# 512-column products in two feed-forward parts, five table blocks held in the gates' buffer, and new row and request rates in a three-layer transformer kernel

## The chip, the cores and the metric

One core of one Trainium2 chip runs the whole program in one launch. The metric is the device time of that core in microseconds (us); lower is better.

## The reference, cut to what matters

256 tokens of width 1024 pass through three blocks: a convolution and attention mix followed by a layer of 16384 small experts (called peer), then an attention mix with a feed-forward part, then a gating and attention mix with a second feed-forward part. All of it is float32. Of the parts the change touches:

```python
def chunk(args):
    hx, idx, g = args
    a = jax.nn.gelu(jnp.einsum("ced,cd->ce", u_emb[idx], hx), approximate=False)
    return jnp.einsum("ce,ced->cd", g * a, v_emb[idx])
...
h = _rmsnorm(x, norm_ffn[layer])
gu = h @ ffn_w_gu[layer]
x = x + (jax.nn.silu(gu[..., :FFN_HIDDEN]) * gu[..., FFN_HIDDEN:]) @ ffn_w_down[layer]
```

Each token has 128 chosen experts (8 heads, 16 each); u_emb and v_emb have 16384 rows of 1024. FFN_HIDDEN is 2816, which is 22 chunks of 128.

## The kernel before, in words

**Products.** Activations are kept with features on the partitions, a chunk being 128 features by 256 tokens. A weight tile of 128x1024 (512 KB, `raw`) holds eight 128x128 blocks. ScalarE rounds it to `whi` (line 150), VectorE (line 157) or, early in the program, GpSimd (line 155) takes the remainder `wlo`. The activations are split in the same way into a high and a low tile. `mm_t` (lines 176 to 178) makes three products of 256 columns for each block: `whi` with the high activations, `whi` with the low ones, `wlo` with the high ones, all summed in one PSUM tile. The program has four such PSUM tiles (`mm`) and four others (`ax`). `token_major` (lines 242 to 244) is the other way round: 128 tokens are the stationary operand and 512 columns of a weight tile stream past.

**Feed-forward parts** (`ffn`, one per later layer). For each of 22 chunks f the kernel makes two such sums of eight blocks, the gate `pg` and the up part `pu`. Then `act` scales both by the norm `rb` from PSUM (lines 1421 and 1423), applies Silu on ScalarE (1422), multiplies (1424) and splits the result into `ah` and `al` (387, 388). The first part multiplies by the down weights in `residual`, eight sums of 22 blocks each; the second uses `token_major`, in `finish`. Weights come by DMA from SyncE's queue (SP), line 130.

**The peer layer.** The first 160 tokens are computed densely: all 128 blocks of the first table `ut` (line 1054, 16 matmuls a block, `ublock`), gelu into a buffer G, a product of one-hot matrices placed over G by `place` and `put` (lines 1092, 1102), then all 128 blocks of the second table `vv` (line 1162, 16 matmuls a block, `vmm`), the upper 64 first. G is two tiles of 64 x 160 columns. For the last 96 tokens, in two groups (`RowGroup`, 64 and 32 indices wide), GpSimd gathers rows: 96 indirect DMAs of 512 KB from `un` (the first table), each followed by a dot product on VectorE (line 1653), and 96 from `vv`, each followed by a scaled addition (line 1663). Eight row buffers serve them, so a gather waits until the arithmetic on the row eight before it is done. `some_rows(r)` advances the gathers by r per table block: `RU` per block of the first table, `RV` per block of the second.

**Where blocks live.** The first eight `ut` blocks go to the row buffers, asked for by ScalarE before the stage. The others go through a ring of ten 512 KB buffers (`whole`, line 1042), in order of a running number, and SP asks for each as soon as the buffer's earlier block has been multiplied. Of the second table's blocks every fourth by that number is asked for by GpSimd instead, in GpSimd's program order among the gathers; the first of them is the very first block of the second table. The order of this stage on each engine is the order in which the code is written (`in_order`).

Of the kernel before, what the change touches and what calls it, by code (L numbers as in the profile page):

```python
# [9 lines left out]
F32 = mybir.dt.float32  # L10
F32R = mybir.dt.float32r
# [3 lines left out]
AF = mybir.ActivationFunctionType  # L15
# [7 lines left out]
T = 256  # L23
D = 1024
C = D // 128
# [57 lines left out]
QP = 2.8  # L83
UP = (1.5, 1.3)

RU = 0.85
RV = 0.78

AL = 1
GL = (4, 6, 8)  # L90
# [3 lines left out]
N = ROWS[-1][0]  # L94

RB = 8


class Kernel:
# [80 lines left out]
    def wblocks(self):  # L180
        while True:
            for hi, lo in self.blocks(1):
                for b in range(8):
                    yield hi, lo, b

    def mm_tile(self):
        return self.pp.tile([128, T], F32, name="mm", bufs=4)

    def chunk(self, xs, kc=8, order=None):
        pt = self.mm_tile()  # L190
        self.mm_t(self.wb, xs, order or range(kc), pt, (True, True))
        self.tick()
        return pt
# [35 lines left out]
    def token_major(self, xs, kc, n, last=1, first=None, each=None):  # L229


        nc = self.nc
        xh, xl = xs
        pts = [self.pp.tile([128, n], F32, name="mm", bufs=4) for _ in range(2)]
        per = 1024 // n

        def part(tt, t0, hi, lo):
            for j in range(per):
                k = t0 * per + j
                s = slice(j * n, (j + 1) * n)  # L240
                ts = slice(tt * 128, (tt + 1) * 128)
                nc.tensor.matmul(pts[tt], xh[:, k, ts], hi[:, s], start=(k == 0), stop=False)  # L242
                nc.tensor.matmul(pts[tt], xl[:, k, ts], hi[:, s], start=False, stop=False)  # L243
                nc.tensor.matmul(pts[tt], xh[:, k, ts], lo[:, s], start=False, stop=(k == kc - 1))  # L244

        nt = kc // per
        for t0 in range(nt - last):
            (hi, lo), = self.blocks(1)
            for tt in range(2):
                part(tt, t0, hi, lo)  # L250
            self.tick()
            if each:
                each()
        ends = list(self.blocks(last))
        for tt in range(2):
            for t0, (hi, lo) in enumerate(ends):
                part(tt, nt - last + t0, hi, lo)
            if tt == 0 and first:
                first(pts[0])
        for _ in ends:  # L260
            self.tick()
        return pts
# [138 lines left out]
        self.later(1, scale)  # L401
        self.later(2, rows)

    def residual(self, pool, chunk, old, g):

        nc = self.nc
        x = pool.tile([128, C, T], F32, name="x")
        xh = pool.tile([128, C, T], F32R, name="xgh")
        xl = pool.tile([128, C, T], F32R, name="xgl")
        rb = pool.tile([128, T], F32, name="rb")  # L410
        r = self.token_scale()
        step, sums = self.squares(pool, "sq")
        for c in range(C):
            pt = chunk(c)
            nc.vector.tensor_add(x[:, c], pt, old[:, c])
            nc.scalar.activation(xh[:, c], x[:, c], AF.Copy, scale=self.p(g, c))
            nc.vector.scalar_tensor_tensor(xl[:, c], x[:, c], self.p(g, c), xh[:, c], op0=ALU.mult, op1=ALU.subtract)
            step(c, x[:, c])
        self.norm_later(r, rb, sums, D)
        return x, (xh, xl), r, rb  # L420


    def attention(self, pairs):
# [418 lines left out]
    def peer(self):  # L842
        nc, a = self.nc, self.a
        p2h, p2t, p2q = self.p2h, self.p2t, self.p2q
        x, xs, r, rb = self.x, self.xs, self.r, self.rb
# [18 lines left out]
        pr = self.open("rows", side="right")  # L864
        first = [pr.tile([128, D], F32, name="row", bufs=RB) for _ in range(RB)]
        for i, raw in enumerate(first):
# [101 lines left out]
        for h in range(8):  # L968
            for c in range(2):
                pt = self.chunk(xs)  # L970
# [52 lines left out]
        pg = self.open("pg", side="right")  # L1023
        Gs = [pg.tile([128, 64, N], F32, name="G0")]
# [4 lines left out]
        def some_rows(n):  # L1029
            nonlocal owed  # L1030
            owed += n
            while owed >= 1.0:
                owed -= 1.0
                next(fetch, None)

        ring = ["raw", "whi", "wlo", "raw", "whi", "wlo", "raw", "whi", "wlo", "raw"]

        def whole(src, n, eng=nc.sync):

            name = ring[n % len(ring)]  # L1040
            raw = self.sp.tile([128, 1024], F32, name=name, bufs=ring.count(name))
            eng.dma_start(raw, src)
            return raw
# [4 lines left out]
        muls = []  # L1048

        def ublock(i, n_t):  # L1050
            raw = first[i] if i < RB else whole(a["ut"][i], i - RB)
            pt = self.pp.tile([128, N], F32, name="mm", bufs=4)
            for k in range(C):
                nc.tensor.matmul(pt, raw[:, k * 128:(k + 1) * 128], hn[:, k, :N], start=(k == 0), stop=(k == C - 1))  # L1054
            self.tick()
            if n_t == 0:
                nc.scalar.activation(G(i), pt, AF.Gelu)
            else:
                ac = pg.tile([128, N], F32, name="ac", bufs=3)
                nc.scalar.activation(ac[:, :n_t], pt[:, :n_t], AF.Gelu)  # L1060
                if n_t < N:
                    nc.scalar.activation(G(i, slice(n_t, N)), pt[:, n_t:], AF.Gelu)
                muls.append((G(i, slice(0, n_t)), ac[:, :n_t]))
# [45 lines left out]
        k = next((k for k, u in enumerate(self.bg) if k and u not in firsts), len(self.bg))  # L1109
# [4 lines left out]
        i = 0  # L1114
        while self.bg or self.lag:
            ublock(i, 0)
            self.pump(UP[len(asked)])
            if asked:
                some_rows(RU)
            i += 1  # L1120
# [9 lines left out]
        for g in range(n_g):  # L1130
            if g + 2 < n_g:
                ohs.append(onehots(4 * (g + 2), poh, io))
            while i < i0 + 1 + (g + 1) * (126 - i0) // n_g:
                ublock(i, 4 * done)
                some_rows(RU)
                products(1)
# [5 lines left out]
        while i < 128:  # L1142
            ublock(i, 4 * done)
            if pts:
                put(4 * done, i + 1, pts.pop(0))
                done += 1
            some_rows(RU)
            products(1)
# [15 lines left out]
        for q in range(4):  # L1164
            for k in range(4):
                nc.tensor.matmul(acc[q].rearrange("p a b -> p (a b)")[:, k * 128:(k + 1) * 128], zero, zero, start=True, stop=False, skip_group_check=True)
        nv = 128 - RB
        for i in range(64, 128):

            blk = (i, whole(a["vv"][i], nv, nc.gpsimd if nv % 4 == 0 else nc.sync))  # L1170
            nv += 1
            for d in range(8):
                vmm(blk, d)
            some_rows(RV)
        self.close("pgb")
# [3 lines left out]
        xh = p3h.tile([128, C, T], F32R, name="xgh")  # L1179
        xl = p3h.tile([128, C, T], F32R, name="xgl")  # L1180
        rb = p3h.tile([128, T], F32, name="rb")
        for i in range(64 - LAST):

            blk = (i, whole(a["vv"][i], nv, nc.gpsimd if nv % 4 == 0 else nc.sync))
            nv += 1
            for d in range(8):
                vmm(blk, d)
            some_rows(RV)
        for _ in fetch:
# [40 lines left out]
        r1, r2, r = self.token_scale(), self.token_scale(), self.token_scale()  # L1230
# [177 lines left out]
    def ffn(self, name):  # L1408
        nc = self.nc
        x, xs, rb = self.x, self.xs, self.rb  # L1410
        pf = self.open(name, side=self.side)
        if name == "ffn0f":
            self.odd_rows(pf)
        F = 22
        ah = pf.tile([128, F, T], F32R, name="ah")
        al = pf.tile([128, F, T], F32R, name="al")

        def act(f, pg, pu):
            g = pf.tile([128, T], F32, name="g", bufs=3)
            u = pf.tile([128, T], F32, name="u", bufs=3)  # L1420
            nc.vector.tensor_mul(g, pg, rb)
            nc.scalar.activation(g, g, AF.Silu)
            nc.vector.tensor_mul(u, pu, rb)
            nc.vector.tensor_mul(u, u, g)
            self.split(u, ah[:, f], al[:, f])

        last = name == "ffn1f"
        xt = pf.tile([128, 2, D], F32, name="xt") if last else None

        def turn(tt, half):  # L1430

            pt = self.pp.tile([128, 4, 128], F32, name="ax", bufs=4)
            for k in range(4):
                nc.tensor.transpose(pt[:, k], x[:, 4 * half + k, tt * 128:(tt + 1) * 128], self.ident)
            nc.scalar.activation(xt[:, tt, half * 512:(half + 1) * 512], pt.rearrange("p a b -> p (a b)"), AF.Copy)

        for f in range(F):
            pg = self.chunk(xs)
            pu = self.chunk(xs)
            self.after_norm(lambda f=f, pg=pg, pu=pu: act(f, pg, pu))  # L1440
            if last and f in (8, 10, 12, 14):
                turn(f % 4 // 2, (f - 8) // 4)
        self.flush()
        if last:
            self.finish(pf, (ah, al), F, xt)
            return
        nh = self.next_head(name + "h")
        self.x, self.xs, self.r, self.rb = self.residual(nh, lambda c: self.chunk((ah, al), F), x, "mix1")
        self.dump("x5", self.x)
        self.close(name)  # L1450
        self.close(self.head)
        self.head = name + "h"
# [217 lines left out]
def fetched(groups):  # L1670
# [4 lines left out]
    begun = []  # L1675
    for g, f, s in todo + [(None, 0, 0)] * (RB - 1):
        if g is not None:
# [193 lines left out]
```

## Time and profile before

| what | value |
|---|---|
| median of three runs | 1575.03 us (1572.44 to 1576.2) |
| the profiled execution, its time | 1572.59 us |
| its span | 1570.7 us |
| TensorE busy, share of the span | 1520.5 us, 97% |
| VectorE busy | 1111.3 us, 71% |
| ScalarE busy | 647.5 us, 41% |
| GpSimd busy | 546.5 us, 35% |
| HBM read | 395.04 MB |

PE stands for TensorE's matmuls, DVE for VectorE, ACT for ScalarE, POOL for GpSimd, SP for SyncE, which only asks for transfers. Matmuls overlap in the pipeline, so a busy share of PE near 100% says that it was never empty, and its pace is read from the starts of matmuls that follow each other. In this execution the peer tables are worked on from about 318 to 931 us, the first feed-forward part's gates lie around 1150 us, and the second part's around 1450 us.

### The profile page before, as it was taken

The page shows a single profiled execution, that of the slowest core. Times are in us where ns is not written, and L with a number is a line of the kernel's source. Part 1 is how long each engine was busy: PE and PEld are TensorE (multiplying, and loading weights), DVE is VectorE, ACT ScalarE, POOL GpSimd, SP SyncE. Part 2 cuts the span into 40 slices and gives each one's busy share as a digit, 9 for nine tenths or more (in the row PEclk, how much of TensorE's full clock was granted, in tenths as well). Part 3 has the DMA queues.
Part 4 walks back from the last instruction along what each step waited for, and adds up shares of the span by engine and source line. Part 5 has one row for each costly group of instructions (what it writes and reads, how often), then busy time and mean ns, then how long its engine had stood idle before and what let it go on. Part 6 is the DMA issues. An engine that isn't in the chain of part 4 may idle for free.

```text
span 1570.7 us, 30113 instructions
## 1 busy us (share of the span) xinstructions
PE 1520.5 (97%) x11514; PEld 1462.8 (93%) x11514; DVE 1111.3 (71%) x2510; ACT 647.5 (41%) x1398; POOL 546.5 (35%) x593
## 2 busy tenths in 40 slices
PE   9999988999999998999899999999999999999997
PEld 8988987999999998999899999889999997899986
DVE  6989876979998998544344449777776558776655
ACT  4588454422355542000000034565544446655543
POOL 4957804704587776655455301000000030000000
PEclk9999999999999999999999999999999999999999
DMA  6534547449999999999999955626656586365563
GB/s 201 172 116 128 169 144 277 149 160 366 409 408 408 408 408 405 396 409 409 410 409 408 408 181 184 215 94 197 193 183 187 180 204 190 124 196 177 177 191 115
DMA packets 109680, 399.18 MB, mean 254 GB/s; under 512 B 12516, under 2 KB 12931, under 8 KB 109024
## 3 DMA queue, kind: packets, MB, share of 16 engines
q1 hardware_dynamic: 72720, 262.18, 48.2%
q0 software_dynamic: 35232, 130.64, 21.8%
q10 hardware_dynamic: 1584, 4.45, 0.8%
q8 instruction: 90, 1.47, 0.4%
q14 instruction: 54, 0.44, 0.1%
HBM read 395.04 MB, written 6.11 MB: 255 GB/s over the span
## 4 chain that ended last, share of the span: by engine, by line
PE 81%; DMA 10%; DVE 4%; issue 2%; POOL 1%; ACT 1%; ACTq 0%; POOLq 0%; DVEq 0%
PE mm L1054 17%; PE mm L176 14%; PE mm L178 13%; PE mm L177 13%; PE ax L1162 12%; DMA row<-vv,idx 3%; DMA whi<-vv 2%; DMA raw<-wst 2%; PE mm L244 2%; PE mm L243 2%; PE mm L242 2%; POOL wlo L155 1%; PE ax L1092 1%; DMA wlo<-vv 1%; DVE wlo L157 1%
## 5 line engine op out<-in xcount | busy, mean ns | idle before, releaser
L150 ACT ACTIVATE whi<-raw 128x1024 fp32r<-128x1024 f32 x275 | 290.5, 1059 | 604.4 <-PE ax L1162 281.9
L157 DVE TENSOR_TENSOR wlo<-raw,whi 128x1024 fp32r<-128x1024 f32 x213 | 262.5, 1235 | 115.0 <-ACT whi L150 110.9
L178 PE MATMUL mm<-xgh,wlo 128*128 128x256 f32 x1064 | 302.5, 284 | 3.7 <-DVE wlo L157 3.7
L176 PE MATMUL mm<-xgh,whi 128*128 128x256 f32 x1064 | 305.6, 287 | 0.0
L177 PE MATMUL mm<-xgl,whi 128*128 128x256 f32 x1064 | 302.1, 284 | 0.0
L1663 DVE SCALAR_TENSOR_TENSOR acc<-row,w,acc 128x1024 f32<-128x1024 f32 x94 | 120.8, 1285 | 153.1 <-DMA row<-vv,idx 152.8
L178 PEld LDWEIGHTS mm<-xgh,wlo 128*128 128x128 f32 x1064 | 204.9, 193 | 4.3 <-DVE wlo L157 3.9
L155 POOL TENSOR_TENSOR wlo<-raw,whi 128x256 fp32r<-128x256 f32 x248 | 180.4, 762 | 80.7 <-ACT whi L150 80.4
L176 PEld LDWEIGHTS mm<-xgh,whi 128*128 128x128 f32 x1064 | 204.8, 193 | 2.2 <-issue 1.5
L177 PEld LDWEIGHTS mm<-xgl,whi 128*128 128x128 f32 x1064 | 204.9, 193 | 0.2
L1648 POOL DMA_INDIRECT row<-vv,idx x96 | 127.0, 1323 | 99.7 <-DMA row<-vv,idx 71.0
L1162 PE MATMUL ax<-G,raw 128*128 128x160 f32 x816 | 122.2, 303 | 7.1 <-DMA raw<-vv 7.1
L1648 POOL DMA_INDIRECT row<-un,idx x96 | 110.6, 1153 | 38.6 <-DVE a L1653 18.3
L1162 PEld LDWEIGHTS ax<-G,raw 128*128 128x128 f32 x816 | 115.4, 193 | 7.4 <-DMA raw<-vv 7.4
L1653 DVE CUSTOM_DVE_ANT_0 junk<-row,h 128x1024 f32<-128x1024 f32 x96 | 120.0, 1250 | 0.4
L1054 PE MATMUL mm<-hn,raw 128*128 128x160 f32 x768 | 112.6, 300 | 0.0
L1054 PEld LDWEIGHTS mm<-hn,raw 128*128 128x128 f32 x768 | 106.3, 190 | 0.0
L177 PE MATMUL mm<-hl,whi 128*128 128x256 f32 x368 | 104.3, 283 | 0.0
L1162 PE MATMUL ax<-G,whi 128*128 128x160 f32 x624 | 95.9, 304 | 6.8 <-DMA whi<-vv 6.7
L630 DVE SCALAR_TENSOR_TENSOR ax<-u,cw,ax 128x256 f32<-128x256 f32 x227 | 99.3, 483 | 1.6 <-ACT ax L628 0.8
L1162 PEld LDWEIGHTS ax<-G,whi 128*128 128x128 f32 x624 | 89.6, 194 | 7.5 <-DMA whi<-vv 7.5
L1162 PE MATMUL ax<-G,wlo 128*128 128x160 f32 x608 | 90.8, 301 | 2.5 <-DMA wlo<-vv 2.5
(437 smaller groups left out, 3302.7 us busy)
## 6 DMA issues: line engine op xcount, KB each, us to landing
raw<-wst SPq DMA_DIRECT2D x278, 512.0 KB, 3.7
raw<-ut SPq DMA_DIRECT2D x48, 512.0 KB, 15.7
raw<-vv SPq DMA_DIRECT2D x38, 512.0 KB, 7.9
whi<-ut SPq DMA_DIRECT2D x36, 512.0 KB, 16.0
wlo<-ut SPq DMA_DIRECT2D x36, 512.0 KB, 15.7
whi<-vv SPq DMA_DIRECT2D x33, 512.0 KB, 7.8
wlo<-vv SPq DMA_DIRECT2D x26, 512.0 KB, 7.9
raw<-vv POOLq DMA_DIRECT2D x13, 512.0 KB, 17.0
```

Of the source, the lines that this page charges most:

```text
L150: nc.scalar.activation(hi, raw, AF.Copy)
L155: nc.gpsimd.tensor_sub(lo[:, p], raw[:, p], hi[:, p])
L157: self.pin = nc.vector.tensor_sub(lo, raw, hi)
L176: nc.tensor.matmul(pt, w[:, s], xs[0][:, k], start=first, stop=False)
L177: nc.tensor.matmul(pt, w[:, s], xs[1][:, k], start=False, stop=False)
L178: nc.tensor.matmul(pt, lo[:, s], xs[0][:, k], start=False, stop=last)
L630: nc.vector.scalar_tensor_tensor(y[:, c] if k == 30 else ps, u[:, c, k:k + T], cw[:, c, k:k + 1], ps, op0=ALU.mult, op1=ALU.add)
L1054: nc.tensor.matmul(pt, raw[:, k * 128:(k + 1) * 128], hn[:, k, :N], start=(k == 0), stop=(k == C - 1))
L1162: nc.tensor.matmul(acc[d // 2][:, d % 2, :N], raw[:, d * 128:(d + 1) * 128], G(i), start=False, stop=False, skip_group_check=True)
L1648: self.k.nc.gpsimd.indirect_dma_start(t, None, table, bass.IndirectOffsetOnAxis(ap=self.idx[:, s:s + 1], axis=0))
L1653: self.k.nc.vector.tensor_tensor_reduce(junk, row, self.h, 1.0, 0.0, ALU.mult, ALU.add, self.a[:, s:s + 1])
L1663: self.k.nc.vector.scalar_tensor_tensor(self.acc, row, w, self.acc, op0=ALU.mult, op1=ALU.add)
```

## The change

Four edits. In the feed-forward parts the high and low activations lie side by side (`both`), and `chunk_wide` makes, for each weight block, one product of 512 columns (`whi` with both halves) and one of 256 (`wlo` with the high half). The low half's sum then stands in its own 256 columns of the PSUM tile, and is added behind: by a ScalarE copy and a VectorE addition for `pg` and for `pu`, and by one more VectorE addition for each down chunk of the first part. The second part's `finish` is as before. In the peer layer, blocks 27 to 31 of the first table are asked for by ScalarE at block 2 and lie in the upper half of the first G tile, which is written only from block 32 on; the ring's running number skips them. `RU` goes from 0.85 to 0.90 and `RV` from 0.78 to 0.73. GpSimd asks for no block among the second table's first ten; with the new numbers its first is block 13 of that table.

```diff
-RU = 0.85
-RV = 0.78
+RU = 0.9
+RV = 0.73
 RB = 8
+XB = range(27, 27 + 32 * N // D)
...
+    def chunk_wide(self, xs, kc=8):
+        nc = self.nc
+        pt = self.pp.tile([128, 2, T], F32, name="mm", bufs=4)
+        for k in range(kc):
+            w, lo, b = next(self.wb)
+            s = slice(b * 128, (b + 1) * 128)
+            nc.tensor.matmul(pt.rearrange("p a b -> p (a b)"), w[:, s], xs[2][:, k].rearrange("p a b -> p (a b)"),
+                             start=(k == 0), stop=(k == kc - 1), skip_group_check=True)
+            nc.tensor.matmul(pt[:, 0], lo[:, s], xs[0][:, k], start=False, stop=(k == kc - 1), skip_group_check=True)
+        self.tick()
+        return pt
+    def both(self, pool, n):
+        x = pool.tile([128, n, 2, T], F32R, name="xhl")
+        return x[:, :, 0], x[:, :, 1], x
...
-    def residual(self, pool, chunk, old, g):
+    def residual(self, pool, chunk, old, g, wide=False):
...
+            if wide:
+                nc.vector.tensor_add(old[:, c], pt[:, 1], old[:, c])
+                pt = pt[:, 0]
             nc.vector.tensor_add(x[:, c], pt, old[:, c])
...
+        hold = Gs[0].rearrange("p i t -> p (i t)")[:, 32 * N:]
+        nb = 0
...
-            raw = first[i] if i < RB else whole(a["ut"][i], i - RB)
+            nonlocal nb
+            if i < RB:
+                raw = first[i]
+            elif i in XB:
+                raw = hold[:, (i - XB[0]) * D:(i - XB[0] + 1) * D]
+            else:
+                raw = whole(a["ut"][i], nb)
+                nb += 1
+            if i == 2:
+                for j in XB:
+                    nc.scalar.dma_start(hold[:, (j - XB[0]) * D:(j - XB[0] + 1) * D], a["ut"][j])
...
-        nv = 128 - RB
+        nv = nb
         for i in range(64, 128):
-            blk = (i, whole(a["vv"][i], nv, nc.gpsimd if nv % 4 == 0 else nc.sync))
+            blk = (i, whole(a["vv"][i], nv, nc.gpsimd if nv % 4 == 0 and i >= 64 + len(ring) else nc.sync))
...
-            nc.vector.tensor_mul(g, pg, rb)
+            nc.scalar.activation(g, pg[:, 1], AF.Copy)
+            nc.vector.tensor_add(g, pg[:, 0], g)
+            nc.vector.tensor_mul(g, g, rb)
             nc.scalar.activation(g, g, AF.Silu)
-            nc.vector.tensor_mul(u, pu, rb)
+            nc.scalar.activation(u, pu[:, 1], AF.Copy)
+            nc.vector.tensor_add(u, pu[:, 0], u)
+            nc.vector.tensor_mul(u, u, rb)
             nc.vector.tensor_mul(u, u, g)
...
-            pg = self.chunk(xs)
-            pu = self.chunk(xs)
+            pg = self.chunk_wide(xs)
+            pu = self.chunk_wide(xs)
```

Where the two tables meet, GpSimd's order before is this (`un` and `vv` behind `row` are the tables of the gathers, `R` is a one-hot product, and `raw`, `whi`, `wlo` are ring buffers that take blocks of the second table):

```order
L1082 TENSOR_TENSOR R<-QO,gTl 128x512
L1648 DMA row<-un,idx_4404 128x1024 x6
L1648 DMA row<-vv,idx_4395 128x1024
L1042 DMA raw<-vv 128x1024
L1648 DMA row<-vv,idx_4395 128x1024 x3
L1042 DMA whi<-vv 128x1024
```

and after the change this:

```order
L1688 DMA row<-un,idx_4403 128x1024 x2
L1119 TENSOR_TENSOR R<-QO,gTl 128x512
L1688 DMA row<-vv,idx_4394 128x1024 x16
L1069 DMA wlo<-vv 128x1024
L1688 DMA row<-vv,idx_4394 128x1024 x3
L1069 DMA wlo<-vv 128x1024
```

Before, one gather from the second table stood ahead of GpSimd's first block; now sixteen stand there.

In the first feed-forward part, one chunk f on VectorE read before (`wlo` is a weight remainder, `mm` a PSUM sum, `rb` the norm):

```order
L1421 TENSOR_TENSOR g_12577<-mm_12515,rb_11054 128x256
L157 TENSOR_TENSOR wlo_12620<-raw_12617,whi_12619 128x1024
L1423 TENSOR_TENSOR u_12578<-mm_12546,rb_11054 128x256
L1424 TENSOR_TENSOR u_12578<-u_12578,g_12577 128x256
L157 TENSOR_TENSOR wlo_12659<-raw_12656,whi_12658 128x1024
L388 TENSOR_TENSOR al_11299<-u_12578,ah_11298 128x256
```

and now reads:

```order
L1458 TENSOR_TENSOR g_12233<-mm_12187,g_12233 128x256
L1459 TENSOR_TENSOR g_12233<-g_12233,rb_11047 128x256
L158 TENSOR_TENSOR wlo_12307<-raw_12304,whi_12306 128x1024
L1462 TENSOR_TENSOR u_12234<-mm_12210,u_12234 128x256
L1463 TENSOR_TENSOR u_12234<-u_12234,rb_11047 128x256
L1464 TENSOR_TENSOR u_12234<-u_12234,g_12233 128x256
L158 TENSOR_TENSOR wlo_12330<-raw_12327,whi_12329 128x1024
L408 TENSOR_TENSOR xhl_11291<-u_12234,xhl_11291 128x256
```

Two additions from PSUM have joined the six operations of a chunk, and the order of the others is the same.

On ScalarE the five new requests stand near the start of the first table (`G` is the buffer, line 1094 the gelu of a block):

```order
L1094 ACT_TABLE_LOAD
L1094 ACTIVATE G_4391<-mm 128x160 x2
L1088 DMA G_4391<-ut 128x1024 x5
L1094 ACTIVATE G_4391<-mm 128x160 x14
L1019 ACT_TABLE_LOAD
```

They come behind the gelu of blocks 0 and 1 and ahead of that of block 2.

## Rows read from the trace of the kernel before

**Rows 1.** The page: the span, and the busy time of two engines.
```profile
span 1570.7 us, 30113 instructions
...
PE 1520.5 (97%) x11514; PEld 1462.8 (93%) x11514; DVE 1111.3 (71%) x2510; ACT 647.5 (41%) x1398; POOL 546.5 (35%) x593
```

**Rows 2.** Timeline of PE in the first feed-forward part: start us, length us, what.
```profile
1150.11 0.28 PE L176 MATMUL mm<-xgh,whi 128*128 128x256 f32 x1
...
1150.47 0.28 PE L176 MATMUL mm<-xgh,whi 128*128 128x256 f32 x1
```

**Rows 3.** Timeline of PE in the last product, 512 columns a matmul.
```profile
1528.41 0.39 PE L242 MATMUL mm<-whi,ah 128*128 128x512 f32 x1
...
1529.09 0.39 PE L242 MATMUL mm<-whi,ah 128*128 128x512 f32 x1
```

**Rows 4.** Groups by line on DVE, 1115 to 1195 us: count | busy us, mean ns.
```profile
L157 DVE TENSOR_TENSOR wlo<-raw,whi 128x1024 fp32r<-128x1024 f32 x28 | 34.3, 1225 | 9.3 <-ACT whi L150 8.4
...
L1421 DVE TENSOR_TENSOR g<-mm,rb 128x256 f32<-128x256 f32 x14 | 6.0, 425 | 4.1 <-PE mm L178 4.1
```

**Rows 5.** Timeline of DVE in the same place, with the idle time before each.
```profile
1151.75 0.42 DVE L1421 TENSOR_TENSOR g<-mm,rb 128x256 f32<-128x256 f32 x1 [0.29 <-PE mm L178]
1152.77 1.23 DVE L157 TENSOR_TENSOR wlo<-raw,whi 128x1024 fp32r<-128x1024 f32 x1 [0.60 <-ACT whi L150]
1154.63 0.42 DVE L1423 TENSOR_TENSOR u<-mm,rb 128x256 f32<-128x256 f32 x1 [0.63 <-PE mm L178]
...
1157.51 0.42 DVE L1421 TENSOR_TENSOR g<-mm,rb 128x256 f32<-128x256 f32 x1 [0.29 <-PE mm L178]
```

**Rows 6.** Windows in the peer layer: busy us by engine, PE clock, DMA share, GB/s.
```profile
326.00:341.00 15.00, 15.00 (x114) 15.00 (x114) 13.79 (x58) 4.69 (x11) 0.61 (x2) 1.00 0.01 2
...
371.00:381.00 10.00, 10.00 (x76) 10.00 (x75) 9.24 (x45) 1.44 (x5) 4.06 (x6) 1.00 1.02 408
...
620.00:640.00 20.00, 12.87 (x83) 12.62 (x82) 17.33 (x25) 0.59 (x3) 12.40 (x11) 0.83 0.99 378
890.00:904.00 14.00, 14.00 (x104) 14.00 (x104) 6.42 (x5) 0.00 (x0) 2.02 (x2) 1.00 1.03 408
```

**Rows 7.** Waits of PE from 612 to 932 us: total us, times, longest.
```profile
PE ax L1162 <- DMA raw<-vv: 7.1, 1, 7.1
PE ax L1162 <- DMA whi<-vv: 6.7, 2, 4.1
PE ax L1162 <- DMA wlo<-vv: 2.5, 2, 1.8
```

**Rows 8.** The chain of waits from 560 to 910 us: start us, length us, what.
```profile
603.13 4.40 PE mm L1054 x32
607.53 0.46 PE ax L1092 x8
...
618.55 12.57 DMA raw<-vv
...
872.42 17.35 DMA wlo<-vv
...
889.81 20.28 PE ax L1162 x146
```

**Rows 9.** The page, DMA issues: count, KB each, median us from issue to landing.
```profile
raw<-ut SPq DMA_DIRECT2D x48, 512.0 KB, 15.7
raw<-vv SPq DMA_DIRECT2D x38, 512.0 KB, 7.9
...
raw<-vv POOLq DMA_DIRECT2D x13, 512.0 KB, 17.0
```

**Rows 10.** Timeline of PE in the second table, one block and the next.
```profile
843.10 2.34 PE L1162 MATMUL ax<-G,wlo 128*128 128x160 f32 x16
845.27 1.52 PE L1162 MATMUL ax<-G,raw 128*128 128x160 f32 x10
```

**Rows 11.** Groups by line on DVE, 450 to 610 us: the row dot products.
```profile
L1653 DVE CUSTOM_DVE_ANT_0 junk<-row,h 128x1024 f32<-128x1024 f32 x57 | 69.4, 1217 | 0.0
```

More of the change, by code (lines that the diff above doesn't have):

```diff
@@ L232, in token_major @@
         nc = self.nc
-        xh, xl = xs
+        xh, xl = xs[:2]
         pts = [self.pp.tile([128, n], F32, name="mm", bufs=4) for _ in range(2)]
@@ L402, in norm_later @@
         self.later(2, rows)
-    def residual(self, pool, chunk, old, g):
+    def residual(self, pool, chunk, old, g, wide=False):
         nc = self.nc
         x = pool.tile([128, C, T], F32, name="x")
-        xh = pool.tile([128, C, T], F32R, name="xgh")
-        xl = pool.tile([128, C, T], F32R, name="xgl")
+        xh, xl, xb = self.both(pool, C)
         rb = pool.tile([128, T], F32, name="rb")
@@ L419, in residual @@
         self.norm_later(r, rb, sums, D)
-        return x, (xh, xl), r, rb
+        return x, (xh, xl, xb), r, rb
     def attention(self, pairs):
@@ L1414, in ffn @@
         F = 22
-        ah = pf.tile([128, F, T], F32R, name="ah")
-        al = pf.tile([128, F, T], F32R, name="al")
+        ah, al, ab = self.both(pf, F)
         def act(f, pg, pu):
@@ L1447, in ffn @@
         nh = self.next_head(name + "h")
-        self.x, self.xs, self.r, self.rb = self.residual(nh, lambda c: self.chunk((ah, al), F), x, "mix1")
+        self.x, self.xs, self.r, self.rb = self.residual(nh, lambda c: self.chunk_wide((ah, al, ab), F), x, "mix1", True)
         self.dump("x5", self.x)
```

## The prediction

> **What bounds the kernel now.** I read the page first: PE is busy 97% of the span [rows 1]. So time can be gained where PE's own work shrinks, or where PE waits. Two stretches matter, and a different view answers for each.
>
> In the feed-forward parts the timeline of PE is a comb without gaps. The first of three products of one weight block starts at 1150.11 and the first of the next block at 1150.47 [rows 2], so three products of 256 columns take 0.360 us, 0.120 each. PE is the limit there, and only a smaller bill for PE helps. The last product of the kernel already streams 512 columns: three starts lie between 1528.41 and 1529.09 [rows 3], 0.227 us each. That is less than twice 0.120. Solved for a price per column and one per matmul, the two spacings give 0.417 ns a column and 13.3 ns for each instruction.
>
> In the peer layer the windows show transfers that hardly run from 326 to 341 us (2 GB/s) while PE multiplies blocks it already has, and then 408 GB/s from 371 on [rows 6]. A block or a gathered row is 512 KB, 0.524 MB, so one takes 0.524/408 = 1.285 us of all transfers: I call that a unit. The waits of PE by line are 16.3 us, all on blocks of the second table [rows 7]: 7.1 on its first block and 9.2 later. The chain of waits says which blocks: the first was asked for only at 618.55 and took 12.57 us; the last such wait ends at 889.81, for a block asked for at 872.42 that took 17.35 us [rows 8]. Those are GpSimd's: a block that SP asks for lands in 7.9 us, one that GpSimd asks for in 17.0 [rows 9], with gathers queued ahead of it.
>
> **The change part by part.**
>
> *512-column products.* A weight block costs 0.227 + 0.120 = 0.347 us of PE in place of 0.360. Gates and up parts have 2 x 22 x 2 x 8 = 704 blocks, the first part's down product 8 x 22 = 176, together 880. 880 x 0.0133 = **11.7 us**. Bounds: nothing is gained if a 512-column product costs two of 256 here; the weight block is swapped at every matmul in both combs, so I take the measured 0.227. The Trainium skill ("TensorE: Matmul & The Clock Gate", section "Back-to-back issue gap") gives N/2.4 + 2.5 ns for a warm gap, which would make the saving 2.5 ns a block, 2.2 us in all. It speaks against this change, but it would put 256 columns at 109 ns and 512 at 216, and the rows have 120 and 227, so I go by the rows.
>
> *What this adds on ScalarE and VectorE.* A chunk f lasts 5.76 us now (1151.75 to 1157.51 [rows 5]) and 16 x 0.347 = 5.55 after. VectorE works 2 x 1.225 + 4 x 0.425 = 4.15 us in it [rows 4] and gets two more additions of that size: 5.00 of 5.55. ScalarE has two weight roundings and two small operations, and gets two copies; it stays well under VectorE. So both hide under PE, by 0.55 us on VectorE. If that cover went, every 0.1 us of a longer round would cost 44 x 0.1 = 4.4 us. VectorE now idles 0.29, 0.60 and 0.63 us a round at three points [rows 5], waiting for PE and ScalarE; those waits are slack of an engine that is ahead, and should be filled. The eight extra additions of the down product lie in chunks of 22 x 0.347 = 7.6 us and cost nothing; the one behind the last chunk is covered by seven weight blocks of the next product.
>
> *Five blocks held.* ScalarE asks for them behind the gelu of block 1, at about 322 us (two blocks of 2.2 us after the table begins). Five requests hold ScalarE up for a few us; four PSUM tiles of 2.2 us each cover that. The transfers, 5 x 1.285 = 6.4 us, fall into the idle window up to 341 us. From 371 us on the transfers have 6.4 us less to bring. While blocks 27 to 31 are used no ring buffer comes free, so SP asks for nothing for 11 us; gathers and the 15.7 us that a block of this table is in flight [rows 9] keep the transfers busy, narrowly. **6.4 us** less transfer, which counts only if transfers set the end.
>
> *They do.* With PE alone the second table costs 845.27 - 843.10 = 2.17 us a block [rows 10], 8.7 us for four. Four blocks and 4 x 0.78 rows are 7.12 units, 9.15 us: transfers are slower, and PE's lead is eaten until it waits. After the change four blocks and 4 x 0.73 rows are 6.92 units, 8.89 us, still over 8.7, and still at 408 GB/s at 890 to 904 us [rows 6].
>
> *Row rates.* 0.05 more for some 112 blocks of the first table is six gathers earlier, and six fewer later. In the first table two blocks and the one-hot products behind them take PE 4.40 + 0.46 us [rows 8], 2.43 us a block; 1.90 units are 2.44 us. So the first table now needs all transfers, and the 6.4 us of blocks held pay for the six rows (7.7 us). VectorE does 57 dots of 1.217 us in 160 us there with no wait ahead of them [rows 11]; three to four more are 4 to 5 us, which I take to fit. Cost: nothing, but no gain either except through the next step.
>
> *SP asks for the first ten.* The 7.1 us wait at the seam goes: SP can ask for the first block as soon as a buffer is free, some 20 us before it is needed. The transfers lost 20 x (1 - 378/408) = **1.5 us** there [rows 6]. What is late next is GpSimd's first block, now block 13: sixteen gathers stand ahead of it, of which 13 x 0.73, nine to ten, come after the seam. At 1.285 us each with SP's blocks between them, up to 2.57 us, GpSimd asks some 12 to 25 us after the seam and the block lands 17 us later, 29 to 42; PE wants it after 13 x 2.17 = 28. So the wait moves to block 13, 1 to 14 us.
>
> *What the peer layer gains.* As transfers are busy all the time, such waits do not add up; the end follows from what must be delivered before GpSimd's last late block. That was block 112 with seven gathers behind it (landed 889.81); it becomes block 113, also with seven behind it. One more block to deliver, one block less of PE's work behind it: 2.17 - 1.285 = 0.9 us. Sum 6.4 + 1.5 + 0.9 = **8.8 us**. Bounds: nothing (the new wait starves the transfers as long as the old one did, and the held blocks are lost) and 16.3 (all waits gone).
>
> **Sum.** 11.7 + 8.8 = 20.5 us. The profiled execution took 1572.59 us (span 1570.7), so 1552.1; its time lies 2.4 us under the median of the runs shown, 1575.03, so the median should be **1554.5 us**, 1.3% less.
>
> **The rivals.**
> 1. *GpSimd's block 13 is too late, and it is not made up.* While PE waits, SP's ring is full, only eight gathers are in flight, and each new one needs POOL. If 5 to 6 us of transfer time are lost there, the peer layer gives 3 us: 1560. For it: the sixteen gathers; against: eight gathers are 10 us of queued transfers. 15%.
> 2. *All waits vanish*, because rows and blocks now balance: 16.3 + 11.7, 1547. Against: 8.89 is over 8.7. 7%.
> 3. *The held blocks come when transfers are busy* (ScalarE late), or SP's pause lets the transfers run dry: 6.4 us less gain, 1561. 5%.
> 4. *The wide product costs as much as two*, so that edit does nothing: 0 to 2.2 us instead of 11.7, 1564 to 1566. The two combs speak against it. By the formula of the Trainium skill cited above it would be 1564. 4%.
> 5. *VectorE sets the feed-forward round: slower than before.* If its 1.52 us of waits [rows 5] stay where they are, because each new addition waits for a ScalarE copy that waits for PE, a round is 5.00 + 1.52 = 6.52 us, 0.97 over PE's 5.55, and 44 rounds lose 43 us: 1597. It decides from 5.55 on, and the whole change turns slower from 5.55 + 20.5/44 = 6.02 us a round. Against: those waits are an idle engine's, and a late VectorE meets its inputs ready; the weight remainders are made two tiles ahead. 3% for slower than before, and 7% for a round between 5.55 and 6.02 (1556 to 1574).
>
> **How the numbers follow.** My forecast has 59%: 1551 to 1558 by the spread of the runs shown and the 1.5 and 0.9 us terms. The range 1546 to 1564 takes in rivals 1 to 3 and the upper part of 5, some 85%. A measurement of this kernel can tell about 0.2%, 3 us, from no change. Faster by more than that: the forecast, rivals 1 to 4 and most of the 7%, 0.94. Within: 0.02. Slower: rival 5 and what I don't see, 0.04.
>
> **What would show it.** In the profile after: starts in the gates alternating 0.227 and 0.120, no idle PE there, VectorE near 90% in that stretch; transfers at work between 326 and 341 us; no wait at the seam, a wait before block 13, and the later waits smaller; the second table's end near 922 us instead of 931, and the first part's gates about 5 us shorter. A round of VectorE over 5.55 us with PE waiting, or a second table that ends at 928 or later, would prove the matching term wrong.

## The result, and the profile after

The changed kernel takes 1563.98 us (median of 5 runs, 1562.55 to 1566.71) beside 1576.2 us of the kernel before in the same runs: ratio 0.9934, 95% interval [0.9918, 0.995]. By the ratio that is 10.4 us less (7.9 to 12.9), by the two medians 12.2; the forecast was 20.5. The profiled execution took 1563.79 us, 8.8 under that of before.

The page:
```profile
span 1562.0 us, 28572 instructions
...
PE 1517.8 (97%) x10634; PEld 1414.2 (91%) x10634; DVE 1138.7 (73%) x2606; ACT 665.3 (43%) x1486; POOL 542.8 (35%) x590
```
Matmuls are 880 fewer than in [rows 1], one for each block, but PE's busy time fell by only 2.7 us; two steps of the sum have to be looked at apart.

**The gates.** Windows of the kernel after in the first part's gates (busy us of PE, PEld, DVE, ACT, POOL, then clock, DMA share, GB/s), and the same stretch before:
```profile
1100.00:1200.00 100.00, 100.00 (x567) 86.87 (x566) 85.22 (x147) 59.22 (x109) 0.00 (x0) 1.00 0.63 191
```
```profile
1100.00:1200.00 100.00, 100.00 (x835) 100.00 (x835) 71.78 (x106) 49.81 (x71) 0.00 (x0) 1.00 0.60 188
```
PE is busy in all 100 us, at a granted clock of 1.00 (2.4 GHz). VectorE rose from 72% to 85% and ScalarE from 50% to 59%: the additions are hidden. But PE's timeline (start us, length us) shows another spacing than forecast:
```profile
1149.96 0.40 PE L195 MATMUL mm<-xhl,whi 128*128 128x512 f32 x1
1150.20 0.28 PE L197 MATMUL mm<-xhl,wlo 128*128 128x256 f32 x1
1150.31 0.40 PE L195 MATMUL mm<-xhl,whi 128*128 128x512 f32 x1
...
1151.02 0.40 PE L195 MATMUL mm<-xhl,whi 128*128 128x512 f32 x1
```
From 1149.96 to 1151.02 lie three blocks, 1.06 us: 0.3533 a block, not 0.3467. Of the 0.0133 us that a block was to save, half is there, in this execution.

**The peer layer.** The same windows as [rows 6] and two that follow them, after:
```profile
326.00:341.00 15.00, 15.00 (x114) 15.00 (x113) 13.76 (x59) 4.79 (x11) 0.84 (x2) 1.00 0.48 176
371.00:381.00 10.00, 10.00 (x75) 10.00 (x75) 9.28 (x46) 1.40 (x5) 3.29 (x6) 1.00 1.03 409
390.00:402.00 12.00, 12.00 (x91) 12.00 (x90) 11.56 (x32) 1.82 (x6) 4.77 (x5) 1.00 0.87 284
402.00:414.00 12.00, 12.00 (x90) 12.00 (x89) 11.48 (x27) 4.39 (x8) 5.49 (x5) 1.00 1.00 397
620.00:640.00 20.00, 19.61 (x142) 18.77 (x141) 14.03 (x16) 0.59 (x3) 11.46 (x11) 1.00 1.03 408
```
and the two that were not shown of before:
```profile
390.00:402.00 12.00, 12.00 (x91) 12.00 (x90) 11.45 (x34) 1.83 (x6) 4.54 (x5) 1.00 1.03 409
402.00:414.00 12.00, 12.00 (x90) 12.00 (x90) 11.58 (x25) 4.40 (x8) 5.42 (x6) 1.00 1.03 410
```
The held blocks did fall into the idle window (174 GB/s more for 15 us, 2.6 MB). But from 390 to 414 us the transfers ran dry: (409 - 284) x 12 + (410 - 397) x 12 is 1.66 MB given back. What is left is 0.95 MB, 2.3 us at 408 GB/s, not 6.4. At the seam 378 GB/s became 408, 0.6 MB or 1.5 us, as forecast. Together 3.8 us; the second table's last product starts 4.1 us earlier (at 925.57 against 929.65; each is the second product of its row, after and before):
```profile
925.43 0.43 PE L1199 MATMUL ax<-G,wlo 128*128 128x160 f32 x2
```
```profile
929.51 0.43 PE L1162 MATMUL ax<-G,whi 128*128 128x160 f32 x2
```
The two spans differ by 8.7 us (1570.7 and 1562.0): 4.1 up to that product, and 4.6 behind it, where of the change only the wide products lie. The first table begins at 317.8 us in both.

PE's waits from 612 to 932 us, to be held against [rows 7], and the chain of waits there (start us, length us), against [rows 8]:
```profile
PE ax L1199 <- DMA raw<-vv: 4.9, 7, 1.3
PE ax L1199 <- DMA wlo<-vv: 2.9, 3, 2.4
PE ax L1199 <- DMA whi<-vv: 0.6, 2, 0.4
```
```profile
638.56 19.56 DMA wlo<-vv
658.16 10.65 PE ax L1199 x64
...
861.83 17.52 DMA whi<-vv
879.39 32.05 PE ax L1199 x234
```
The waits halved, from 16.3 to 8.4 us (10.6 in run 12's profile), and the end moved by 4.1. The wait at the seam is gone; the longest is now the one before block 13, 2.4 us, for a block that GpSimd asked for at 638.56 and that took 19.56 us. The last wait ends at 879.39 and not at 889.81, before block 109 (868.0, where block 104 starts, and five of 2.17 us).

DMA issues (count, KB each, median us from issue to landing):
```profile
raw<-ut SPq DMA_DIRECT2D x46, 512.0 KB, 11.8
raw<-vv SPq DMA_DIRECT2D x40, 512.0 KB, 8.1
...
G<-ut ACTq DMA_DIRECT2D x5, 512.0 KB, 5.3
```
A block of the first table is in flight for 11.8 us where it was 15.7 [rows 9]. The backlog that was to cover SP's pause was used up in it: SP's queue has no request between those at 381.75 and 394.79 us.

### The profile page after: what moved, and what is told of

Read it like the earlier page. It is cut to its first block, busy times and chain, and to the rows that moved or that the text cites. A ratio compares the mean times of both kernels' runs of the same rounds, so it can differ in the third digit from the quotient of the medians.

```text
span 1562.0 us, 28572 instructions
## 1 busy us (share of the span) xinstructions
PE 1517.8 (97%) x10634; PEld 1414.2 (91%) x10634; DVE 1138.7 (73%) x2606; ACT 665.3 (43%) x1486; POOL 542.8 (35%) x590
## 4 chain that ended last, share of the span: by engine, by line
PE 79%; DMA 12%; DVE 5%; issue 2%; ACT 1%; POOL 1%; ACTq 0%; POOLq 0%; DVEq 0%
PE mm L1091 18%; PE mm L195 13%; PE ax L1199 9%; PE mm L177 7%; PE mm L179 7%; PE mm L178 7%; PE mm L197 7%; DMA raw<-vv 5%; DMA wlo<-vv 3%; PE mm L264 2%; DMA raw<-wst 2%; PE mm L263 1%; PE mm L262 1%; DVE wlo L158 1%; PE ax L1129 1%
## 5 line engine op out<-in xcount | busy, mean ns | idle before, releaser
L195 PE MATMUL mm<-xhl,whi 128*128 128x512 f32 x880 | 311.7, 400 | 0.0
L197 PE MATMUL mm<-xhl,wlo 128*128 128x256 f32 x880 | 247.4, 281 | 0.0
L195 PEld LDWEIGHTS mm<-xhl,whi 128*128 128x128 f32 x880 | 165.5, 188 | 39.9
L197 PEld LDWEIGHTS mm<-xhl,wlo 128*128 128x128 f32 x880 | 166.7, 189 | 0.2
L1091 PE MATMUL mm<-hn,raw 128*128 128x160 f32 x736 | 106.5, 301 | 0.0
L1199 PE MATMUL ax<-G,wlo 128*128 128x160 f32 x624 | 95.9, 304 | 3.3 <-DMA wlo<-vv 2.9
L1199 PEld LDWEIGHTS ax<-G,wlo 128*128 128x128 f32 x624 | 88.0, 192 | 5.3 <-DMA wlo<-vv 5.2
L1199 PE MATMUL ax<-G,whi 128*128 128x160 f32 x608 | 90.8, 301 | 1.1 <-DMA whi<-vv 0.6
L177 PE MATMUL mm<-hh,whi 128*128 128x256 f32 x304 | 88.5, 291 | 0.0
L179 PE MATMUL mm<-hh,wlo 128*128 128x256 f32 x304 | 87.0, 286 | 0.5 <-POOL wlo L156 0.4
## 6 DMA issues: line engine op xcount, KB each, us to landing
raw<-ut SPq DMA_DIRECT2D x46, 512.0 KB, 11.8
wlo<-ut SPq DMA_DIRECT2D x34, 512.0 KB, 11.7
```

Of the source, the lines that this page charges most:

```text
L177: nc.tensor.matmul(pt, w[:, s], xs[0][:, k], start=first, stop=False)
L179: nc.tensor.matmul(pt, lo[:, s], xs[0][:, k], start=False, stop=last)
L195: nc.tensor.matmul(pt.rearrange("p a b -> p (a b)"), w[:, s], xs[2][:, k].rearrange("p a b -> p (a b)"), start=(k == 0), stop=(k == kc - 1 ...
L197: nc.tensor.matmul(pt[:, 0], lo[:, s], xs[0][:, k], start=False, stop=(k == kc - 1), skip_group_check=True)
L1199: nc.tensor.matmul(acc[d // 2][:, d % 2, :N], raw[:, d * 128:(d + 1) * 128], G(i), start=False, stop=False, skip_group_check=True)
```

## The experiments

Theory A, formed on this profile: an alternating block costs 0.353 us, because each change between 512 and 256 columns costs something, and of the held blocks' 6.4 us some 4 are lost again. Theory B is the prediction as it stood.

**1. The wide products alone.** The change without its peer-layer edits (here and below, - is the change and + the experiment):
```
-XB = range(27, 27 + 32 * N // D)
+XB = range(27, 27)
-RU = 0.9
-RV = 0.73
+RU = 0.85
+RV = 0.78
-... nc.gpsimd if nv % 4 == 0 and i >= 64 + len(ring) else nc.sync
+... nc.gpsimd if nv % 4 == 0 else nc.sync
```


> The kernel before with the 512-column products alone; no block is held, and the row and request rates are the old ones. Theory A (read from the profile after the change): a 512-column and a 256-column product that alternate take 0.353 us a weight block, not 0.347, so 880 blocks save 5.9 us: ratio to before 0.9963, with starts 0.233 to 0.241 and 0.113 to 0.120 apart. Theory B (the prediction): 11.7 us, ratio 0.9926; whatever is missing after the change then went elsewhere.

Measured: 1569.56 us, ratio 0.9956 [0.9939, 0.9973], 6.9 us less (4.3 to 9.6). Nearer to A. But the profile holds something that neither expects: the first part runs at one spacing, the second at the other. PE's timeline near 1150 us:
```profile
1149.92 0.40 PE L195 MATMUL mm<-xhl,whi 128*128 128x512 f32 x1
...
1150.96 0.39 PE L195 MATMUL mm<-xhl,whi 128*128 128x512 f32 x1
```
and near 1470 us, in the second part:
```profile
1470.07 0.40 PE L195 MATMUL mm<-xhl,whi 128*128 128x512 f32 x1
...
1471.13 0.40 PE L195 MATMUL mm<-xhl,whi 128*128 128x512 f32 x1
```
Three blocks each: 1.04 us, then 1.06, from the same line in one execution.

**2. The peer layer alone.** The change with feed-forward parts and residual as before (256 columns, three products a block).

> The kernel before with the peer layer's three edits alone and the old products. Theory A: the transfers run short of requests at 390 to 414 us, so the held blocks are worth 2.4 us of the 6.4, and the three edits 4 to 5 us: ratio 0.997. Theory B (the prediction): 8.8 us, ratio 0.9944.

Measured: 1572.27 us, ratio 0.9969 [0.9959, 0.998], 4.9 us less (3.2 to 6.5). The prediction's 8.8 is out; the dip is there again.

**3. Products of one length grouped.**
```
-for k in range(kc): 512 columns of block k; 256 columns of block k
+for each weight tile: 512 columns of its 8 blocks; then 256 columns of the same 8
```


> The changed kernel with the products of a weight tile in another order: all its 512-column products first (up to eight), then all its 256-column ones. Theory A (a change of length costs some 7 ns a weight block): within a run of equal length the starts are 0.227 and 0.120 apart, a block costs about 0.348, and the time falls by 880 x 0.0058 = 5 us below the changed kernel, ratio to before about 0.990. Rival (a 512-column product with these operands costs 0.236 wherever it stands): no difference from the changed kernel, ratio 0.993.

Measured: 1562.52 us, ratio 0.9903 [0.9885, 0.992]. PE's timeline over one tile:
```profile
1152.32 2.00 PE L199 MATMUL mm<-xhl,whi 128*128 128x512 f32 x8
1154.16 1.12 PE L203 MATMUL mm<-xhl,wlo 128*128 128x256 f32 x8
1155.12 0.86 PE L199 MATMUL mm<-xhl,whi 128*128 128x512 f32 x3
```
From 1152.32 to 1155.12 are eight blocks, some 0.350 us each; nearly all whole tiles have 0.349. The time is what A gave, but run 12 shows that A's reason is not the right one, and 0.350 lies between the two spacings of the alternating order. Of the 4.9 us between the two ratios the spacing can explain 3 to 4 at most (880 x 0.0033 to 0.0043); I don't call this kernel faster than the change.

**4. No block held.** `XB` empty, the rest as changed.

> The changed kernel without held blocks; all blocks go through the ring. Theory A: 2.4 us slower than the changed kernel, ratio to before about 0.995, and no dip of the transfers at 390 to 414 us. Theory B (the prediction's 6.4 us): ratio about 0.9975.

Measured: 1566.53 us, ratio 0.9937 [0.9919, 0.9954]: 2.5 us over the change by the medians, 0.5 by the ratios, so the times alone can't tell it from the change. The dip is gone, as A has it:
```profile
390.00:402.00 12.00, 12.00 (x91) 12.00 (x90) 11.55 (x32) 1.82 (x6) 4.79 (x5) 1.00 1.03 408
```
but the first table, whose 0.9 rows a block need all transfers, now waits (PE 1.6 us), and its last product starts at 627.0 us instead of 621.8 (624.1 in run 12, the changed kernel again). Clearer is the length of the peer layer in the profiles, from the first table's first product to the second table's last: 612.4 us here, and 607.8 to 609.2 in the four profiles with the change's peer layer (the change, runs 2, 3 and 12). With these rates the held blocks are worth 3.2 to 4.6 us by that, more than the 2.3 that the bytes gave and less than the 6.4 of the prediction.

**5. The rates undone.** `RU = 0.85`, `RV = 0.78`.

> The change with only the two rates put back to 0.85 and 0.78 rows a block. Transfers set the end (theory): some six gathers move behind the seam, where four blocks and their rows are 7.12 units of transfer in place of 6.92, and each costs up to 1.28 us there, while the first table only gains idle transfers: the second table ends 3 to 7 us later, 1567 to 1571 us, ratio to before 0.996 to 0.998. Rival (the rates are nothing, since transfers or VectorE already make up for it in the first table): same as the change, 1564 us, ratio 0.993.

Measured: 1567.76 us, ratio 0.9949 [0.9935, 0.9962]; 3.8 us over the change by the medians, 2.4 by the ratios, whose intervals overlap. The peer layer lasts 611.4 us in this profile, 2.2 to 3.6 over those four profiles. So the rates earn something, at the theory's lower end or just under it.

**6. GpSimd asks among the first ten again.** The condition on `i` taken out.

> The change with only GpSimd's share of the second table's first ten blocks given back to it (three of the first ten). Theory: PE waits some 5 to 8 us at the second block of the second table in place of 2.7 us at block 13, but the waits do not add up; only the lull of the transfers at the seam returns, 1 to 2 us: 1565 to 1566 us, ratio 0.994. Rival (each wait counts in full): the 7 us wait at the seam comes back on top of the rest, 1570 us, ratio 0.997. Second rival (the edit costs as much at block 13 as it gives at the seam): 1564 us or less.

Measured: 1564.8 us, ratio 0.9929 [0.9916, 0.9942]: no difference that can be told. Yet PE waits longer at one place than in any other run:
```profile
PE ax L1199 <- DMA raw<-vv: 11.7, 5, 9.2
```
9.2 us at the table's second block, and the end is the same within 1 us; the peer layer lasts 609.1 us. That wait did not count. The lull did not return either (405 GB/s from 620 to 640 us, where run 1, with GpSimd asking for the very first block, has 377). So this run doesn't test the 1.5 us of the seam, which are read from the windows alone.

**7. More gathers during SP's pause.**
```
-some_rows(RU)
+some_rows(RU + (0.8 if i in XB else 0))
-RV = 0.73
+RV = 0.7
```


> The change with four more gathers asked for while the five held blocks are used (1.7 in place of 0.9 rows for each of them), and 0.70 rows a block in the second table. Theory (SP's pause starves the transfers): the windows between 390 and 414 us stay at 400 GB/s or more, the 4 us of transfers lost there come back, the second table ends 3 to 4 us earlier, 1560 us, ratio 0.9908. Rival (VectorE is the limit where rows are scored in the first table): transfers stay busy, but rows wait for VectorE and PE for them, no gain or up to 5 us lost, 1564 to 1569 us.

Measured: 1568.79 us (1561.01 to 1570.79), ratio 0.9946 [0.9926, 0.9966]. The theory's remedy failed: 276 GB/s from 390 to 402 us, and no gain. PE's waits in the first table, of which the change has none:
```profile
PE ax L1032 <- DVE ex L1024: 4.9, 1, 4.9
```
VectorE, busy 11.66 of 12 us in that window, came late with the softmax, and GpSimd's gathers waited for its dot products, up to 2.6 us at a time. So rows could not fill the pause here; that VectorE is why is read from these waits and not tested.

**8. Twelve gathers left out.**
```
+... if not (f and s % 8 == 7)
-RV = 0.73
+RV = 0.63
```


> Leaves out 12 of the second table's 96 gathered row groups (every eighth) and what they add to the sum, with 0.63 rows a block there. Theory (transfers set the end of the second table): 12 units of 1.28 us are 15 us less to bring; the 12 us of small waits that PE has there vanish but for 2 us, so some 10 us less, 1554 us, ratio 0.987. Rival (PE and the latency of GpSimd's requests set the end, transfers do not): waits stay within 3 us, 1561 to 1564 us, ratio 0.991 to 0.993.

Measured: 1553.21 us, ratio 0.9856 [0.984, 0.9872], 10.8 us under the change. PE's waits from 600 to 932 us:
```profile
PE ax L1199 <- DMA raw<-vv: 1.6, 4, 0.7
PE ax L1199 <- DMA wlo<-vv: 0.6, 2, 0.4
```
The waits are 2.2 us in place of 8.4, the peer layer lasts 597.3 us, at least 10.5 less, and from 640 to 820 us every window of 60 us still reads 407 to 409 GB/s (409 in the change). Fewer bytes, an earlier end: transfers do set the second table's end. The run takes 12 requests from GpSimd's queue as well; that those are not the cause rests on run 11, where SP alone asks for the late blocks and the end stays.

**9 to 11. The gathers later.** If transfers stand idle after 905 us, rows could go there. First 0.63 rows a block up to block 108, then 1.45; then the same with grouped products; then 0.65 up to block 100, 1.08 after, and SP alone asking from block 97 on.

> The change with the second table's gathers shifted to its end: 0.63 rows a block for the first 108 blocks, 1.45 for the last 15, in place of 0.73 throughout; the same rows in all. Theory (transfers set the end, and those of the last 20 us, from 905 us on, stand idle because the ring of ten blocks has been filled): ten or eleven gathers go into that idle time, four blocks with their rows are 6.52 units, 8.38 us, under PE's 8.7, so the waits shrink to a few us as in the run with 12 gathers left out: 8 to 11 us less, 1553 to 1556 us, ratio 0.986 to 0.988. Rival (the late gathers hold up GpSimd's last blocks or the adding up of rows on VectorE, behind which the stage ends): waits near blocks 109 to 128 of as much as is gained, 1562 to 1568 us.

> The change with both: the 512-column products of a weight tile ahead of its 256-column ones, and the gathers shifted as above. If the two are independent, the gains add: 1551 to 1554 us, ratio 0.982 to 0.986, faster than both kernels. If the late gathers give nothing: that of the grouping alone, 0.990.

> As the run with late gathers, but milder (0.65 rows a block for the first 100 blocks of the second table, 1.08 for the next 23), and SP alone asks for the blocks from the 97th on, so that no block stands behind the late gathers in GpSimd's order. Theory (transfers set the end; what cost the run with late gathers its gain was only that GpSimd's blocks 113, 117 and 121 stood behind them): those three waits of 2.3 to 3.4 us and their half clock go, PE works almost without a wait from 630 us to the end of the table, 6 to 10 us less than the change, 1554 to 1558 us, ratio 0.985 to 0.989. Rival (whoever asks, blocks among so many gathers come too late): waits of 5 to 10 us after block 100, no gain over the change, 1563 us or more.

Measured: 1565.75 us, ratio 0.9926 [0.9909, 0.9943]; 1566.02 us, 0.9932 [0.9919, 0.9945]; 1564.16 us, 0.9929 [0.9915, 0.9943]. My theory fell three times. In the first, PE works almost without a wait up to 878 us (some 2 us in all), and then stands before blocks 113, 117 and 121 (PE's timeline; in brackets the idle time before):
```profile
880.86 3.43 PE L1200 MATMUL ax<-G,wlo 128*128 128x160 f32 x16 [2.04 <-DMA wlo<-vv]
894.42 3.35 PE L1200 MATMUL ax<-G,wlo 128*128 128x160 f32 x16 [2.93 <-DMA wlo<-vv]
908.15 1.08 PE L1200 MATMUL ax<-G,raw 128*128 128x160 f32 x6 [3.09 <-DMA raw<-vv]
```
In the last, those three are gone, and PE waits just behind them, for the last five blocks (windows):
```profile
890.00:900.00 10.00, 10.00 (x75) 10.00 (x75) 4.98 (x4) 0.00 (x0) 0.00 (x0) 1.00 1.03 410
900.00:905.00 5.00, 1.81 (x12) 1.32 (x10) 2.33 (x3) 0.00 (x0) 0.00 (x0) 0.98 0.87 342
905.00:910.00 5.00, 3.15 (x10) 2.35 (x11) 1.68 (x2) 0.00 (x0) 0.00 (x0) 0.50 0.40 161
```
The same bytes have to land, so moving rows moves PE's waits and brings the end no earlier (the peer layer lasts 611.1, 611.4 and 608.6 us in the three profiles); here PE also dropped to a granted clock of 0.50, 1.2 GHz, behind a window in which it worked 1.81 of 5 us. Grouping added nothing to the late rows (0.9932 beside 0.9926). That decides little, for in the profile of run 9 most alternating blocks took 0.3467 anyway.

**12. The changed kernel again.**

> The changed kernel once more, nothing edited. In the traces so far an alternating pair costs either 0.3467 or 0.3533 us for a whole stretch, and the same product code showed both in one execution. Theory (the rhythm is set by where the stream last paused, by chance of the execution): this execution shows at least one stretch of 0.3467 where the first one had 0.3533 throughout, and its runs spread over 4 to 6 us. Rival (the program fixes it, the first execution's 0.3533 is this kernel's own): 0.3533 in every stretch of the gates again.

Measured: 1564.23 us (1561.94 to 1565.92), ratio 0.9924 [0.9912, 0.9937]. Its timeline near 1150 us:
```profile
1150.05 0.39 PE L195 MATMUL mm<-xhl,whi 128*128 128x512 f32 x1
1150.28 0.27 PE L197 MATMUL mm<-xhl,wlo 128*128 128x256 f32 x1
1150.39 0.40 PE L195 MATMUL mm<-xhl,whi 128*128 128x512 f32 x1
...
1151.09 0.40 PE L195 MATMUL mm<-xhl,whi 128*128 128x512 f32 x1
```
Three blocks in 1.04 us: the forecast's 0.3467, from the same program that had 0.3533 before. But for a few blocks it holds up to 1430 us; behind that both occur, and the last stretch, from 1453 us, runs at 0.3533. The program alone does not fix the spacing of the first part, and a change of length has no fixed price: theory A falls here, and B's 0.3467 is one of two values.

Two stretches of the profiles keep the two halves of the change apart (us; the second reaches from the second table's last product to the end of the span):

| profile | peer layer | behind it |
|---|---|---|
| before | 611.9 | 641.0 |
| 1, wide products alone | 613.6 | 633.9 |
| 2, peer layer alone | 609.0 | 640.7 |
| the change | 607.8 | 636.4 |
| 12, the change again | 609.2 | 632.8 |

Each is one execution. The peer layer's edits give 2.7 to 5.8 us by this. Behind it, the ten profiles of the alternating order have 632.8 to 636.4, so the wide products give 4.3 to 8.2.

## Why the prediction was half right

- **PE bounds the gates, and the additions hide under it: right.** PE is busy 100 of 100 us, VectorE 85 (about 90 forecast). Rival 5 is out.
- **A block costs 0.347 us: mis-sized.** The step that failed is adding the steady 512-column spacing to the steady 256-column one, "so I take the measured 0.227". Mixed, the pair settles at 0.3467 or 0.3533. By the spacing the term is 880 x 0.0067 = 5.9 us to 880 x 0.0133 = 11.7, by the execution; alone it measured 6.9 (4.3 to 9.6), and the profiles show 4.3 to 8.2. Some 1 to 4 us that the spacing of each profile promises are not seen there; where they go stays open.
- **The wide product as dear as two (rival 4): out.** The rows had 0.227 and 0.120, and in steady alternation the runs have 0.229 to 0.242 and 0.112 to 0.121. By the formula of the Trainium skill ("TensorE: Matmul & The Clock Gate", "Back-to-back issue gap") the saving would be 2.2 us, an estimate; the page gives that formula for a single matmul in isolation, and run 1, with 6.9 us (4.3 to 9.6), does not agree with it.
- **Held blocks, 6.4 us: wrong.** The step that failed is "gathers and the 15.7 us that a block of this table is in flight [rows 9] keep the transfers busy, narrowly": they did not. This is rival 3's second half, and its 5% was too low. No buffer of SP's ring came free, and what was in flight ended before SP asked again (284 GB/s from 390 to 402 us); more rows did not fill the gap (run 7). By the bytes 2.3 us stayed, by run 4's profile 3.2 to 4.6.
- **The seam: right in place.** The wait went, 378 GB/s became 408, and block 13 waits for GpSimd. Its 2.4 us are not rival 1, for no transfer time was lost with them (409 GB/s from 640 to 700 us). The 1.5 us themselves no run isolates.
- **0.9 us for one block later: wrong.** The last wait is before block 109, not 113, and when PE last waits says little: with transfers as the limit the bytes count. The term is nothing. The second table ended near 927 us, and near 929 in run 12, where 922 was forecast.
- **Transfers set the end: right.** Run 8 (fewer bytes, 10.8 us) and run 6 (9.2 us of wait, no loss) show it from both sides. That the rates pay only with the held blocks fits runs 4 and 5, where either alone has a peer layer of 612.4 and 611.4 us beside 611.9 before; it isn't shown, as no run has neither with the rest as changed.

The sum as the rows afterwards would have it: 3.8 us for the peer layer, 5.9 to 11.7 for the products, 9.7 to 15.5 in all; from 1576.2 that is 1560.7 to 1566.5. The eleven timed runs of the changed program lie between 1561.94 and 1566.71. Between the two profiled executions, 11.8 of the 20.5 us are missing: 4.7 in the peer layer and 7.1 behind it, of which the spacing explains 5.8. The median misses by 9.5 us, 1.2 of them because before itself ran at 1576.2 this time.

## What to carry to other kernels

A spacing that is measured in a stream of equal instructions was the best case here, not the price, for a stream that mixes them: keep a range in the sum. Where a change has two halves, read the length of each stretch from the profiles; the whole time mixes them. Where transfers set the end of a stage, count bytes by windows, those lost as well as those won; waits of the engine behind them move about and don't add up. A prefetch into an idle window is worth only what the transfers can still find to do later: ask who will request anything while the prefetched blocks are in use.

## What was not expected of the hardware

Alternating matmuls of 512 and 256 columns, weights swapped at each, run in one of two steady rhythms at a granted clock of 1.00 (2.4 GHz): starts 229 to 233 and 112 to 118 ns apart (three pairs in 1.04 us), or a cycle of three pairs, 231 to 242 and 112 to 121 ns (1.06 us). The rhythm changes only where other matmuls or a pause come between; in run 5 one pause of 0.17 us, at 1104.9 us, turned 0.3533 into 0.3467. In ten profiles of the alternating order the first part's gates ran four times at 0.3533 and six times (run 5 behind that pause) at 0.3467 us a block. Yet the last stretch of the second part, about 110 blocks, ran at 0.3533 in all ten, so chance is not the whole of it. Grouped by eight, the 512-column starts begin at 233 and 236 ns and settle at 227. What in PE chooses the rhythm stays open.
